# Holding the casts of early summed weights and of the second down group behind bank reads, and giving the down projection two more raw tiles

## The chip, the cores and the metric

The kernel runs on one core of a Trainium2 chip. The metric is the device time of one execution in microseconds, as the median of several runs. One execution was also recorded by the hardware profiler; the views of the profile quoted below come from that one.

## The reference

A two-layer encoder trunk: 1024 tokens of width 1024. Each layer mixes tokens (windowed attention in layer 0, a neighbourhood attention on a grid in layer 1), attends to a fixed memory, and then runs a SwiGLU feed-forward block of width 2816. The change lies in the feed-forward block:

```python
def rmsnorm(x, g):
    x32 = x.astype(jnp.float32)
    y = x32 * lax.rsqrt(jnp.mean(x32 * x32, axis=-1, keepdims=True) + EPS)
    return (y * g.astype(jnp.float32)).astype(x.dtype)
...
    for i in range(DEPTH):
        ...
        x = x + jnp.concatenate([y_tok, y_mem], axis=-1) @ w_out[i]
        h = rmsnorm(x, norm_ffn[i])
        gu = h @ w_gate_up[i]
        x = x + (jax.nn.silu(gu[..., :D_FF]) * gu[..., D_FF:]) @ w_down[i]
    return rmsnorm(x, norm_final)
```

## The kernel before

Activations are kept transposed: 8 tiles of 128 features, each in two token halves of 512 (`HS`). Every operand of a product is split into a high part, rounded by a cast on ACT (`hi`, L107), and the rest, by a subtraction on DVE (`lo`, L110); one product of two such operands is three matmuls (high x high, high x low, low x high).

The feed-forward products use a scheme of seven block products for a two by two block matrix product (products n = 0 to 6). Some of them read plain blocks, others sums and differences of blocks. For the gate and up projection the blocks of the weights are the left sides, those of the normalized activations the right sides:

- `right_sides()` makes `B[3]`, `B[2]`, `B[5]`, `B[4]`, `B[6]` step by step on DVE: normalize (L1291), subtract (L1288), then split into tiles named hT (`t_op`) or hB (`h_op`), four pieces each. `B[0]` and `B[1]` exist earlier.
- `Pair(j)` is a unit of 128 hidden features, j = 0 to 21. `prepare(n)` makes the weight of products n and n + 1: for n = 2 and n = 4 GpSimd forms sums of raw blocks in the tile wS (L1065, L1058), the n = 4 sums in place of the n = 2 sums; then `hi` and `lo` split the result. wS has two buffers, split weights (tag whl, names wgu, later wd) three, raw weights (tag raw) five. `load_gu()`, called by `prepare`, starts the load of a later raw tile on the SP queue.
- `product(n)` issues 12 matmuls into a PSUM bank X or Y (L1101), and `read(n)` takes the bank out: copies on ACT (L1112, L1118, L1121, L1126) or additions on DVE (L1109).
- Product 6 of two neighbouring units from the third pair on is itself split again (`Fourth`, matmuls L1183, reads L1211).

`order` lists the products. The first four units (`first`) run products 0 and 1 first, then two by two 3, 2, 5, 4, 6, each for both units. `gate_up()` walks through it, and prepares `lead` = 4 steps ahead. The scheduler of the framework sets the order on each engine from the code and its own estimates, so an operation of `prepare` may be placed earlier than it is written. Each engine takes its instructions in that order and waits at the first one that isn't ready.

The down projection has the same seven products, in the order 0, 1, 3, 2, 4, 5, 6, over six groups of hidden units (five of two, one of one). `left_side(i, g)` loads, combines and splits the weights of one group (raw tiles named wd_raw, kept blocks wd_kept), two groups ahead; `right_side` does it for the activations (b_raw, hB). Products i = 3 and i = 4 (the fourth and fifth) load two raw blocks and add or subtract them on DVE (L1429, L1435). `read` adds the banks to the residual on DVE (L1496). The dictionary `ahead` starts the first groups while the gate and up products still run: `left_side(0, 1)` three steps before their end.

Of the kernel before, what the change touches and what calls it, by code (L numbers as in the profile page):

```python
# [17 lines left out]
P = 128  # L18
D = 1024
# [22 lines left out]
def trunk_kernel(ctx: ExitStack, tc: tile.TileContext, a: dict, out: bass.AP):  # L42
# [61 lines left out]
        return phase[0].tile([P, D], F32, tag="raw", name=name, bufs=phase[2])  # L104

    def hi(dst, src):
        nc.scalar.copy(dst, src)  # L107

    def lo(dst, src, h, eng=None):
        (eng or nc.vector).tensor_tensor(dst, src, h.bitcast(F32), op=ALU.subtract)  # L110

    def load_w(src, tag="whl", bufs=3, eng=None, name="w", pool=wp, parts=1, raw=None):
        if raw is None:
# [428 lines left out]
    for layer in range(2):  # L542
# [467 lines left out]
        with (  # L1010
# [32 lines left out]
            class Pair:  # L1043


                def __init__(self, j):
                    self.j = j
                    self.left, self.raw, self.seen = {}, {}, set()

                def prepare(self, n):  # L1050

                    n -= n % 2
                    if n in self.left:
                        return
                    g1, g2 = self.raw[0][:, :HS], self.raw[0][:, HS:]
                    if n > 0:
                        u1, u2 = self.raw[1][:, :HS], self.raw[1][:, HS:]
                    sub = lambda o, p_, q_: nc.gpsimd.tensor_tensor(o, p_, q_, op=ALU.subtract)  # L1058
                    s = self.raw[0]
                    if n == 2:  # L1060
                        self.s = fs.tile([P, D], F32, tag="S", name="wS", bufs=2)
                    if n in (2, 4):
                        s = self.s
                    if n == 2:
                        nc.gpsimd.tensor_tensor(s[:, HS:], u1, u2, op=ALU.add)  # L1065
                        sub(s[:, :HS], s[:, HS:], g1)
                    if n == 4:
                        sub(s[:, HS:], g1, u1)
                        sub(s[:, :HS], g2, s[:, :HS])
                    if n == 0 and self.j < first:  # L1070
                        w = fp.tile([P, 2, D], F32R, tag="t8", name="wgu8", bufs=6)
                    elif n == 2 and self.j >= first:
                        w = fp.tile([P, 2, D], F32R, tag="w8", name="wgu2", bufs=1)
                    else:
                        w = wp.tile([P, 2, D], F32R, tag="whl", name="wgu", bufs=3)
                    if n == 6:
                        hi(w[:, 0, :HS], u2)
                        lo(w[:, 1, :HS], u2, w[:, 0, :HS])
                    else:
                        hi(w[:, 0], s)  # L1080
                        lo(w[:, 1], s, w[:, 0])
                    self.left[n], self.left[n + 1] = w[:, :, :HS], w[:, :, HS:]
                    if n == 4:
                        self.left[4], self.left[5] = self.left[5], self.left[4]
                    if n > 3 or (n == 0 and 2 <= self.j < first):
                        load_gu()
# [19 lines left out]
                def read(self, n):  # L1106
                    self.seen.add(n)
                    X, Y = self.X, getattr(self, "Y", None)
                    add = lambda o, p_, q_, op=ALU.add: nc.vector.tensor_tensor(o, p_, q_, op=op)  # L1109
                    if n == 0:  # L1110
                        self.g1 = temp("g1")
                        nc.scalar.copy(self.g1, X)  # L1112
                    elif n == 1:
                        add(self.g1, Y, self.g1)
                        nc.scalar.activation(self.g1, self.g1, AF.Silu)
                    elif n == 2:
                        self.g2 = temp("g2")
                        nc.scalar.copy(self.g2, X)  # L1118
                    elif n == 3:
                        self.c2 = temp("c2")  # L1120
                        nc.scalar.copy(self.c2, Y)  # L1121
                        if 4 in self.seen:
                            add(self.c2, self.c2, self.c1)
                    elif n == 4:
                        self.c1 = temp("c1")
                        nc.scalar.copy(self.c1, X)  # L1126
                        if 3 in self.seen:
                            add(self.c2, self.c2, self.c1)
                        if 5 in self.seen:
                            add(self.c2, self.c2, self.g2, ALU.mult)  # L1130
                    elif n == 5:
                        add(self.g2, Y, self.g2)
                        nc.scalar.activation(self.g2, self.g2, AF.Silu)
                        if 4 in self.seen:
                            add(self.c2, self.c2, self.g2, ALU.mult)
                    else:
                        add(self.c1, self.c1, X, ALU.subtract)
                        add(self.c1, self.c1, self.g1, ALU.mult)
# [3 lines left out]
            class Fourth:  # L1142
# [65 lines left out]
                def read(self, n):  # L1208
                    (a, b), X, Y = self.units, self.X, self.Y
                    low, high = slice(0, h2), slice(h2, HS)  # L1210
                    sub = lambda c, ps, op=ALU.subtract: nc.vector.tensor_tensor(c, c, ps, op=op)  # L1211
                    if n == "A":
                        sub(a.c1[:, low], X[:, low])
                        sub(a.c1[:, low], Y[:, low])
                    elif n == "B":
                        sub(a.c1[:, high], X[:, low])
                        sub(b.c1[:, high], Y[:, high])
                    else:
                        sub(
                            b.c1.rearrange("p (n c) -> p n c", n=2),  # L1220
                            X[:, low].unsqueeze(1).to_broadcast([P, 2, h2]),
                        )
                        sub(b.c1[:, low], X[:, high], ALU.add)
                        sub(b.c1, b.g1, ALU.mult)
                        sub(a.c1[:, high], Y[:, high])
                        sub(a.c1, a.g1, ALU.mult)
# [141 lines left out]
            def gate_up():  # L1368
                load_gu()
                for i, (u, n) in enumerate(order):  # L1370
                    if i + lead < len(order):
                        v, n_ = order[i + lead]
                        v.prepare(n_)
                    u.product(n)
                    u.read(n)
                    if i == 1:
                        norms[1].sums()
                    if i > 1:
                        run_some(rest, 2 if i == 2 or i >= 2 * first else 1)
                    if i >= 7 * first - 1:  # L1380
                        run_some(more, 1)
                    if n == "C":
                        hand_over(u.units[0].j // 2, *u.units)
                    elif n == 6 and u.j % 2:
                        hand_over(u.j // 2, us[u.j - 1], u)
                    yield i - len(order)
# [16 lines left out]
                    kept[g] = fp.tile([P, 2, 2, HS], F32, tag="t8", name="wd_kept", bufs=6)[:, :n]  # L1403
                    rows(kept[g][:, :, 0], g, 0, slice(0, HS))

            def left_side(i, g):

                p, n = groups[g]
                first_cols, second_cols = slice(0, HS), slice(HS, D)

                def raw():
                    return raw_tile("wd_raw").rearrange("p (n c) -> p n c", c=HS)[:, :n]

                if i == 0:
                    keep_rows(g)
# [7 lines left out]
                    nc.vector.tensor_tensor(a, b, a, op=ALU.subtract)  # L1423
                    src = a
                elif i == 3:
                    r, o = raw(), raw()
                    rows(r, g, 0, second_cols)
                    rows(o, g, 1, second_cols)
                    nc.vector.tensor_tensor(b, r, o, op=ALU.add)  # L1429
                    src = b  # L1430
                elif i == 4:
                    src, o = raw(), raw()
                    rows(src, g, 0, first_cols)
                    rows(o, g, 0, second_cols)
                    nc.vector.tensor_tensor(src, src, o, op=ALU.subtract)  # L1435
                elif i == 5:
                    src = raw()
                    rows(src, g, 1, first_cols)
                    nc.vector.tensor_tensor(src, src, a, op=ALU.subtract)
                else:  # L1440
                    src = raw()
                    rows(src, g, 1, second_cols)
                w = wp.tile([P, 2, D], F32R, tag="whl", name="wd", bufs=3)
                hi(two(w[:, 0], n), src)
                lo(two(w[:, 1], n), src, two(w[:, 0], n))
                for q in range(n):
                    left[i, p + q] = w[:, :, q * HS : (q + 1) * HS]

# [145 lines left out]
            }  # L1594
            for to_go in gate_up():
                for what, g in ahead.get(to_go, ()):
                    what(g) if what is keep_rows else what(0, g)
            norms = [Norm(row=None if is_a else next(factor_rows)), Norm()]
            ends = {c: Norm(HS // 2, 7) for c in quarter}
            dorder = [(i, g) for i in (0, 1, 3, 2, 4, 5, 6) for g in range(len(groups))]  # L1600
# [136 lines left out]
```

## Time and profile before

| | us |
|---|---|
| median of 3 runs | 2117.06 |
| lowest and highest | 2116.92, 2117.7 |
| the profiled execution | 2115.94 |
| its span, first to last instruction | 2114.2 |
| PE busy in the span | 2092.7 |
| DVE / ACT / POOL busy | 1524.6 / 1077.9 / 583.6 |

PE is TensorE's matmuls and PEld its weight loads, which run beside them; DVE is VectorE, ACT ScalarE, POOL GpSimd, SP the engine whose queue starts most transfers. The granted clock of TensorE is 0.998 over the span. Busy time counts an instruction from its start to its end and leaves out branches, semaphores and the issuing of transfers. A row of the timeline reads: start, duration, engine, line, operation, output and inputs, shape, count; in brackets the idle time of the engine before it and what ended that. A row of the waits reads: who waited for whom, then the total, how often, and the longest. The gate and up products run from about 393 to 815 us in layer 0 and from about 1466 to 1888 in layer 1, the down projection after them to about 1002 and 2102.

### The profile page before, as it was taken

How to read it: one execution, taken by the hardware profiler on the slowest of the kernel's cores; microseconds unless marked ns; L12 is line 12 of the kernel's file. 1: busy time of each engine (PE TensorE's matmuls, PEld its weight loads, DVE VectorE, ACT ScalarE, POOL GpSimd, SP SyncE). 2: the span in 40 equal slices, each digit the busy share in tenths (PEclk: the TensorE clock that was granted, in tenths of full speed). 3: DMA queues.
4: the chain of work that ended last, by engine and by line, in shares of the span. 5: the costliest groups of instructions: out<-in, count | busy, mean ns of one | idle time of the engine just before them, and what ended most of it. 6: DMA issues, size and time to landing. Idle time of an engine off the chain costs nothing.

```text
span 2114.2 us, 29053 instructions
## 1 busy us (share of the span) xinstructions
PE 2092.7 (99%) x10318; PEld 1750.1 (83%) x10318; DVE 1524.6 (72%) x2474; ACT 1077.9 (51%) x2037; POOL 583.6 (28%) x615
## 2 busy tenths in 40 slices
PE   9999999999999999999999999999999999999998
PEld 8788888888888888888888888888888888888887
DVE  7687886987666667776766666677986666677675
ACT  6687775544434335344466666664543434344443
POOL 0344330334444430000233223203243444400001
PEclk9999999999999999999999999999999999999999
DMA  6421128332333227866232222275232333267662
GB/s 232 146 82 51 36 83 288 99 115 100 110 108 111 91 105 254 313 216 207 78 110 68 69 72 78 64 266 157 75 110 105 110 115 104 91 254 256 205 221 95
DMA packets 121778, 288.08 MB, mean 136 GB/s; under 512 B 12705, under 2 KB 21153, under 8 KB 121633
## 3 DMA queue, kind: packets, MB, share of 16 engines
q1 hardware_dynamic: 113744, 272.42, 38.4%
q10 hardware_dynamic: 7888, 13.79, 1.7%
q8 instruction: 82, 1.34, 0.3%
q14 instruction: 64, 0.52, 0.1%
HBM read 211.19 MB, written 68.95 MB: 133 GB/s over the span
## 4 chain that ended last, share of the span: by engine, by line
PE 80%; issue 12%; DVE 3%; ACT 2%; POOL 2%; DMA 1%; POOLq 0%; ACTq 0%; SPq 0%; DVEq 0%
PE X L1101 16%; PE Y L1101 16%; PE mm L141 15%; PE po L141 8%; PE X L1532 5%; PE Y L1532 4%; PE O L809 3%; PE S L746 3%; PE pT L789 3%; PE X L1183 2%; PE Y L1183 2%; PE mm L448 1%; ACT p L761 1%; POOL wS L1058 1%; POOL wf L110 1%
## 5 line engine op out<-in xcount | busy, mean ns | idle before, releaser
L1101 PE MATMUL Y<-hB,wgu 128*128 128x512 f32 x1056 | 255.5, 391 | 0.8 <-ACT c L1121 0.8
L1101 PE MATMUL X<-hB,wgu 128*128 128x512 f32 x1056 | 254.8, 391 | 0.0
L1532 PE MATMUL X<-hB,wd 128*128 128x512 f32 (+1 forms) x1092 | 243.2, 383 | 0.9 <-DVE x L1496 0.9
L110 DVE TENSOR_TENSOR wgu<-wS,wgu 128x1024 fp32r<-128x1024 f32 (+1 forms) x124 | 155.4, 1253 | 120.9 <-ACT wgu L107 120.7
L1532 PEld LDWEIGHTS X<-hB,wd 128*128 128x128 f32 x1092 | 200.2, 188 | 41.4 <-issue 1.7
L1101 PEld LDWEIGHTS Y<-hB,wgu 128*128 128x128 f32 x1056 | 196.8, 188 | 43.4 <-ACT c L1121 1.6
L1101 PEld LDWEIGHTS X<-hB,wgu 128*128 128x128 f32 x1056 | 196.0, 188 | 39.8
L774 POOL TENSOR_SCALAR p<-p,stat 128x384 f32<-128x384 f32 (+1 forms) x256 | 143.1, 579 | 308.7 <-DVE stat L771 213.4
L141 PE MATMUL mm<-hT,wqk 128*128 128x512 f32 x672 | 199.3, 405 | 0.0
L107 ACT CAST wgu<-wS 128x1024 fp32r<-128x1024 f32 (+1 forms) x124 | 114.3, 923 | 142.0 <-POOL wS L1058 124.6
L141 PE MATMUL po<-yT,wo 128*128 128x512 f32 x768 | 184.2, 393 | 0.0
L1532 PE MATMUL Y<-hB,wd 128*128 128x512 f32 x792 | 180.4, 389 | 0.0
L1532 PEld LDWEIGHTS Y<-hB,wd 128*128 128x128 f32 x792 | 148.6, 188 | 31.2 <-DVE x L1496 0.4
L244 POOL TENSOR_TENSOR nr<-nv,neg_half 128x4 f32<-128x4 f32 (+1 forms) x12 | 13.3, 1105 | 582.9 <-DVE nv L243 573.7
L141 PEld LDWEIGHTS po<-yT,wo 128*128 128x128 f32 x768 | 142.7, 188 | 28.8 <-DVE yT L110 0.2
L1101 PE MATMUL X<-hT,wgu 128*128 128x512 f32 x624 | 150.2, 391 | 0.0
L107 ACT CAST hB<-b_raw 128x512 fp32r<-128x512 f32 x154 | 89.4, 618 | 115.5 <-DMA b_raw<-b_d 100.3
L1058 POOL TENSOR_TENSOR wS<-wgu_raw 128x512 f32<-128x512 f32 x44 | 61.2, 1391 | 292.1 <-DVE wgu L110 292.1
L1101 PEld LDWEIGHTS X<-hT,wgu 128*128 128x128 f32 x624 | 116.8, 188 | 26.3
L761 ACT ACTIVATE p<-p,stat 128x256 f32<-128x256 f32 (+1 forms) x192 | 112.4, 587 | 48.1 <-DVE stat L757 46.0
L110 DVE TENSOR_TENSOR pl<-pT,ph 128x384 fp32r<-128x384 f32 (+1 forms) x256 | 119.0, 493 | 19.1 <-ACT ph L107 15.9
L110 DVE TENSOR_TENSOR hB<-b_raw,hB 128x512 fp32r<-128x512 f32 x154 | 99.9, 687 | 42.2 <-ACT hB L107 42.1
(201 smaller groups left out, 4248.1 us busy)
## 6 DMA issues: line engine op xcount, KB each, us to landing
wgu_raw<-in_w_gu SPq DMA_DIRECT2D x92, 512.0 KB, 3.7
wd_raw<-in_w_dn SPq DMA_DIRECT2D x70, 512.0 KB, 4.4
b_raw<-b_d SPq DMA_DIRECT2D x70, 512.0 KB, 5.4
b_d<-c SPq DMA_DIRECT2D x88, 256.0 KB, 2.1
b_d<-t SPq DMA_DIRECT2D x66, 256.0 KB, 2.2
wo_raw<-in_w_out SPq DMA_DIRECT2D x32, 512.0 KB, 3.5
xr_d<-x ACTq DMA_DIRECT2D x32, 256.0 KB, 2.5
xr<-xr_d SPq DMA_DIRECT2D x16, 512.0 KB, 6.1
```

Source lines behind the costliest of these rows:

```text
L107: nc.scalar.copy(dst, src)
L110: (eng or nc.vector).tensor_tensor(dst, src, h.bitcast(F32), op=ALU.subtract)
L141: nc.tensor.matmul(ps[:, :n], l, r, start=start and i == 0 and j == 0, stop=stop and i == len(order) - 1 and j == 2,)
L746: nc.tensor.matmul(s_[:, :n], Q[self.h][:, qb * P : (qb + 1) * P], k, start=j == 0, stop=j == 1)
L761: nc.scalar.activation(p[:, :n], p[:, :n], AF.Exp, bias=m1, scale=-1.0, accum_out=s1)
L774: nc.gpsimd.tensor_scalar(p[:, :n], p[:, :n], ri[:, i : i + 1], 1.0, op0=ALU.mult, op1=ALU.mult)
L789: nc.tensor.transpose(tr[:, j * P : (j + 1) * P], p[:, j * P : (j + 1) * P], ident)
L809: nc.tensor.matmul(o[:, c0 : c0 + w * P], self.value(j), t[:, s0 : s0 + w].rearrange("p j q -> p (j q)"), start=j == js[0] and t is self.p ...
L1058: sub = lambda o, p_, q_: nc.gpsimd.tensor_tensor(o, p_, q_, op=ALU.subtract)
L1101: nc.tensor.matmul(ps, l, r, start=n in (0, 1, 3, 6) and k == 0 and i == 0, stop=k == 3 and i == 2, skip_group_check=True,)
L1183: nc.tensor.matmul(bank[:, at : at + h2], l, r, start=start and k == 0 and i == 0, stop=stop and k == 1 and i == 2, skip_group_check=True,)
L1532: nc.tensor.matmul(bank[:, c], l, r, start=i in (0, 1, 3, 6) and p == 0 and n == 0, stop=p == HF - 1 and n == 2, skip_group_check=True,)
```

## The change

1. `prepare` is cut in two. GpSimd's sums stay where they were; the split moves into a new function `split(n)`. For the first four units and n = 2 or 4 it is called one step after the sums, and its cast is pinned to its place in the program (`tc.keep_in_program_order`), so that the scheduler doesn't place it earlier. `load_gu()` moves with it.
2. `left_side(0, 1)`, the second group of the down projection, gets a list `behind`: its cast and its subtraction are issued after the last unit's copy of product 4 (`copied`) and after the read of step "B" (`summed`).
3. Products i = 3 and i = 4 of the down projection load their second block into one of two halves of a new tile wd_other (tag w8, the buffer that held the n = 2 weights of the later units) instead of a raw tile. (The product numbers of the short description count from one.)

```diff
     def hi(dst, src):
-        nc.scalar.copy(dst, src)
+        return nc.scalar.copy(dst, src)
...
                     if n == 4:
                         sub(s[:, HS:], g1, u1)
                         sub(s[:, :HS], g2, s[:, :HS])
+                    self.cast[n] = s
+                    if self.j >= first or n not in (2, 4):
+                        self.split(n)
+
+                def split(self, n, pin=False):
+
+                    n -= n % 2
+                    if n not in self.cast:
+                        return
+                    s, u2 = self.cast.pop(n), self.raw.get(1)
...
-                        hi(w[:, 0], s)
+                        ins = hi(w[:, 0], s)
+                        if pin:
+                            tc.keep_in_program_order(ins)
                         lo(w[:, 1], s, w[:, 0])
...
-                        nc.scalar.copy(self.c1, X)
+                        self.copied = nc.scalar.copy(self.c1, X)
...
-                        sub(b.c1[:, high], Y[:, high])
+                        b.summed = sub(b.c1[:, high], Y[:, high])
...
                         v.prepare(n_)
+                        if i >= 2 * first - lead:
+                            v, n_ = order[i + lead - 1]
+                            if v in us[:first]:
+                                v.split(n_, True)
...
+                def other():
+                    t = spare[g % 2].bitcast(F32)
+                    return t.rearrange("p (n c) -> p n c", c=HS)[:, :n]
...
                 elif i == 3:
-                    r, o = raw(), raw()
+                    r, o = raw(), other()
...
                 elif i == 4:
-                    src, o = raw(), raw()
+                    src, o = raw(), other()
...
-                hi(two(w[:, 0], n), src)
-                lo(two(w[:, 1], n), src, two(w[:, 0], n))
+                with ExitStack() as queued:
+                    for ins in behind:
+                        queued.enter_context(tc.issue_after(ins.ins))
+                    hi(two(w[:, 0], n), src)
+                    lo(two(w[:, 1], n), src, two(w[:, 0], n))
...
+                        left_side(0, g, (us[-1].copied, us[-1].summed) if g == 1 else ())
...
+            spare = fp.tile([P, 2, D], F32R, tag="w8", name="wd_other", bufs=1)
+            spare = spare[:, 0], spare[:, 1]
```

The order of PE's matmuls is the same in both kernels. On the other engines it differs at these places.

DVE, at the start of the gate and up products of layer 0 (layer 1 is alike). sq are squares for the norm, st and nv its means, g the gate's output, wgu a split weight, hT a piece of `B[3]` or `B[2]`. Before, ahead of the norm:

```order
L1264 TENSOR_TENSOR x<-po,x 128x512
L110 TENSOR_TENSOR wgu<-wS,wgu 128x1024
L230 TENSOR_TENSOR sq<-sq 128x512 x2
L1109 TENSOR_TENSOR g_4508<-Y,g_4508 128x512
L243 TENSOR_SCALAR nv<-st 128x4
```

and before, while `B[3]` and `B[2]` are made:

```order
L1109 TENSOR_TENSOR g_4602<-Y,g_4602 128x512
L1288 TENSOR_TENSOR x<-x 128x512
L110 TENSOR_TENSOR hT_4580<-x,hT_4580 128x512
L1288 TENSOR_TENSOR x<-x 128x512
L110 TENSOR_TENSOR hT_4631<-x,hT_4631 128x512
L1291 SCALAR_TENSOR_TENSOR x<-x,gains,bc 128x512 x2
```

After, at that second place:

```order
L1121 TENSOR_TENSOR g_4599<-Y,g_4599 128x512
L1300 TENSOR_TENSOR x<-x 128x512
L110 TENSOR_TENSOR hT_4580<-x,hT_4580 128x512
L110 TENSOR_TENSOR wgu<-wS,wgu 128x1024
L110 TENSOR_TENSOR hT_4628<-x,hT_4628 128x512
L1300 TENSOR_TENSOR x<-x 128x512
L110 TENSOR_TENSOR wgu<-wS,wgu 128x1024
L1303 SCALAR_TENSOR_TENSOR x<-x,gains,bc 128x512
```

Three subtractions of summed weights leave the end of the output projection; two of them now stand between the last piece of `B[3]` and the second piece of `B[2]`, the third behind the last piece of `B[2]`.

POOL at the same place. nr belongs to the norm of the second token half. Before:

```order
L1065 TENSOR_TENSOR wS<-wgu_raw 128x512
L1058 TENSOR_TENSOR wS<-wS,wgu_raw 128x512
L1058 TENSOR_TENSOR wS<-wgu_raw 128x512
L1058 TENSOR_TENSOR wS<-wgu_raw,wS 128x512
L1058 TENSOR_TENSOR wS<-wgu_raw 128x512
L1058 TENSOR_TENSOR wS<-wgu_raw,wS 128x512
L1065 TENSOR_TENSOR wS<-wgu_raw 128x512
L1058 TENSOR_TENSOR wS<-wS,wgu_raw 128x512
L244 TENSOR_TENSOR nr<-nv,neg_half 128x4
```

After:

```order
L1065 TENSOR_TENSOR wS<-wgu_raw 128x512
L1058 TENSOR_TENSOR wS<-wS,wgu_raw 128x512
L244 TENSOR_TENSOR nr<-nv,neg_half 128x4
L1058 TENSOR_TENSOR wS<-wgu_raw 128x512
L1058 TENSOR_TENSOR wS<-wgu_raw,wS 128x512
L1058 TENSOR_TENSOR wS<-wgu_raw 128x512
L1058 TENSOR_TENSOR wS<-wgu_raw,wS 128x512
L1065 TENSOR_TENSOR wS<-wgu_raw 128x512
L1058 TENSOR_TENSOR wS<-wS,wgu_raw 128x512
```

The n = 4 sums of the first two units and the n = 2 sum of the third unit, six operations, stand behind the norm instead of ahead of it.

DVE at the end of the gate and up products of layer 1, where the banks X and Y of the last split product 6 are read (c) and the second down group is split (the second wd row). Before:

```order
L110 TENSOR_TENSOR wd<-wd_kept,wd 128x1024
L1211 TENSOR_TENSOR c_17100<-c_17100,X_17220 128x256
L110 TENSOR_TENSOR wd<-wd_kept,wd 128x1024
L1211 TENSOR_TENSOR c_17100<-c_17100,Y_17221 128x256
L1109 TENSOR_TENSOR c_17216<-c_17216,c_17251 128x512
```

After:

```order
L110 TENSOR_TENSOR wd<-wd_kept,wd 128x1024
L1223 TENSOR_TENSOR c_17089<-c_17089,X_17209 128x256
L1223 TENSOR_TENSOR c_17089<-c_17089,Y_17210 128x256
L1121 TENSOR_TENSOR c_17205<-c_17205,c_17240 128x512
L1223 TENSOR_TENSOR c_17089<-c_17089,X_17209 128x256
L1223 TENSOR_TENSOR c_17240<-c_17240,Y_17210 128x256
L110 TENSOR_TENSOR wd<-wd_kept,wd 128x1024
```

The split of the second group has moved behind the four bank reads.

DVE in the down projection of layer 0, where product 2 ends and its banks are read (x). Before:

```order
L1435 TENSOR_TENSOR wd_raw<-wd_raw 128x1024
L110 TENSOR_TENSOR wd<-wd_raw,wd 128x1024
L1496 TENSOR_TENSOR x_00_8736<-X,xr 128x512
L1496 TENSOR_TENSOR x_10_8741<-X,xr 128x512
L1496 TENSOR_TENSOR x_20_8746<-X,xr 128x512
```

After:

```order
L110 TENSOR_TENSOR hB<-b_raw,hB 128x512 x2
L1519 TENSOR_TENSOR x_00_8729<-X,xr 128x512
L110 TENSOR_TENSOR wd<-wd_raw,wd 128x1024
L1519 TENSOR_TENSOR x_10_8734<-X,xr 128x512
L1519 TENSOR_TENSOR x_20_8739<-X,xr 128x512
L1519 TENSOR_TENSOR x_30_8744<-X,xr 128x512
```

The subtraction L1435 (L1455 after) no longer stands ahead of the reads, and the first read precedes the next split.

More of the change, by code (lines that the diff above doesn't have):

```diff
@@ L106, in hi @@
     def hi(dst, src):
-        nc.scalar.copy(dst, src)
+        return nc.scalar.copy(dst, src)
     def lo(dst, src, h, eng=None):
-        (eng or nc.vector).tensor_tensor(dst, src, h.bitcast(F32), op=ALU.subtract)
+        return (eng or nc.vector).tensor_tensor(dst, src, h.bitcast(F32), op=ALU.subtract)
     def load_w(src, tag="whl", bufs=3, eng=None, name="w", pool=wp, parts=1, raw=None):
@@ L1047, in __init__ @@
                     self.j = j
-                    self.left, self.raw, self.seen = {}, {}, set()
+                    self.left, self.raw, self.seen, self.cast = {}, {}, set(), {}
                 def prepare(self, n):
                     n -= n % 2
-                    if n in self.left:
+                    if n in self.left or n in self.cast:
                         return
@@ L1076, in prepare @@
                     if n == 6:
-                        hi(w[:, 0, :HS], u2)
-                        lo(w[:, 1, :HS], u2, w[:, 0, :HS])
-                    else:
-                        hi(w[:, 0], s)
+                        hi(w[:, 0, :HS], u2[:, HS:])
+                        lo(w[:, 1, :HS], u2[:, HS:], w[:, 0, :HS])
+                    else:
+                        ins = hi(w[:, 0], s)
+                        if pin:
+                            tc.keep_in_program_order(ins)
                         lo(w[:, 1], s, w[:, 0])
@@ L1404, in keep_rows, with left_side @@
                     rows(kept[g][:, :, 0], g, 0, slice(0, HS))
-            def left_side(i, g):
+            def left_side(i, g, behind=()):
                 p, n = groups[g]
@@ L1596, in trunk_kernel @@
                 for what, g in ahead.get(to_go, ()):
-                    what(g) if what is keep_rows else what(0, g)
+                    if what is keep_rows:
+                        keep_rows(g)
+                    elif what is left_side:
+                        left_side(0, g, (us[-1].copied, us[-1].summed) if g == 1 else ())
+                    else:
+                        what(0, g)
+            spare = fp.tile([P, 2, D], F32R, tag="w8", name="wd_other", bufs=1)
+            spare = spare[:, 0], spare[:, 1]
             norms = [Norm(row=None if is_a else next(factor_rows)), Norm()]
```

## Prediction

> **What bounds the kernel now.** I read the page first, then the waits of PE and of its weight loads, then windows of the one stretch that the change fills up, then the timeline row by row in it. From the page:
>
> ```profile
> span 2114.2 us, 29053 instructions
> PE 2092.7 (99%) x10318; PEld 1750.1 (83%) x10318; DVE 1524.6 (72%) x2474; ACT 1077.9 (51%) x2037; POOL 583.6 (28%) x615
> ```
>
> PE is busy for 2092.7 of 2114.2 us, so all idle time together is 21.5 us. A change that leaves the matmuls alone can win only the part of it that its own waits hold. The waits of PE that belong to the touched code (total, times, longest), and below them those of the weight loads in front of the same matmuls:
>
> ```profile
> PE Y L1183 <- DVE c L1211: 1.5, 1, 1.5
> PE X L1532 <- DVE x L1496: 0.9, 1, 0.9
> PE Y L1101 <- ACT c L1121: 0.8, 2, 0.4
> ...
> PEld Y L1183 <- DVE c L1211: 1.7, 1, 1.7
> PEld X L1532 <- issue: 1.7, 3, 1.3
> PEld Y L1101 <- ACT c L1121: 1.6, 2, 0.8
> ```
>
> That is 3.2 us by the matmuls, 4.6 us by the weight loads if one takes the longest for X. The share of DVE over the span (72%) hides where it is full. Two windows, one per layer, from the first right side of the second token half to the weight of product 5 of the second unit pair (columns: length, then busy time and instructions of PE, PEld, DVE, ACT, POOL):
>
> ```profile
> 404.35:460.68 56.33, 55.95 (x242) 44.97 (x240) 53.75 (x70) 28.68 (x46) 15.28 (x10) 1.00 0.22 71
> 1476.69:1533.00 56.31, 55.93 (x242) 45.05 (x240) 53.93 (x70) 28.67 (x46) 15.36 (x10) 1.00 0.22 70
> ```
>
> DVE has 56.33 - 53.75 = 2.6 us free in layer 0 and 2.4 in layer 1. The rows at both ends show that PE follows it there:
>
> ```profile
> 423.73 5.76 PE L1101 MATMUL X<-hT,wgu 128*128 128x512 f32 x24
> 425.07 0.69 DVE L110 TENSOR_TENSOR hT<-x,hT 128x512 fp32r<-128x512 f32 x1 [0.64 <-ACT hT L107]
> ...
> 458.98 1.77 DVE L110 TENSOR_TENSOR wgu<-wS,wgu 128x1024 fp32r<-128x1024 f32 x1 [0.69 <-ACT wgu L107]
> 460.81 2.15 PEld L1101 LDWEIGHTS Y<-hB,wgu 128*128 128x128 f32 x10 [0.20 <-DVE wgu L110]
> ```
>
> The first pair: the last piece of right side B[2] is ready at 425.76, and its product, begun at 423.73, needs it with its 11th matmul (10 x 0.24 us later, about 426.1): 0.3 us to spare. The second pair: the weight of that product 5 is ready at 460.75 and the load waits for it. What DVE gets to do on top in this window, beyond its free time, moves PE.
>
> **The early summed weights: DVE work moved into the full window.** Before, three summed weights (twice n = 2, once n = 4) are split while the output projection still runs:
>
> ```profile
> 387.88 1.22 DVE L110 TENSOR_TENSOR wgu<-wS,wgu 128x1024 fp32r<-128x1024 f32 x1
> 394.99 2.15 DVE L110 TENSOR_TENSOR wgu<-wS,wgu 128x1024 fp32r<-128x1024 f32 x1 [0.47 <-ACT wgu L107]
> ...
> 428.08 1.22 DVE L110 TENSOR_TENSOR wgu<-wS,wgu 128x1024 fp32r<-128x1024 f32 x1
> 429.22 1.29 DVE L110 TENSOR_TENSOR hB<-x,hB 128x512 fp32r<-128x512 f32 x2
> ```
>
> After, all three subtractions stand inside the window, two of them ahead of the last piece of B[2]. Each takes 429.22 - 428.08 = 1.14 us of the queue: 3.4 us a layer. The three casts that go with them cost ACT 3 us of a queue that is half idle in the window (28.68 of 56.33): nothing by itself. What leaves the old place is worth little: the subtraction at 394.99 held the last sums of squares, for which the means' weight load waited 0.5 us in layer 0, of which I count 0.3 as an earlier start of the window; layer 1 has no such wait.
>
> ```profile
> PEld st L223 <- DVE sq L230: 0.5, 1, 0.5
> ```
>
> With the casts, GpSimd's sums move. The n = 4 sums overwrite the tile that the n = 2 split reads, so they cannot begin before it is done. Before, six GpSimd operations (both n = 4 sums and the n = 2 sum of the third unit, first and last quoted) ran ahead of the window:
>
> ```profile
> 389.18 1.68 POOL L1058 TENSOR_TENSOR wS<-wgu_raw 128x512 f32<-128x512 f32 x1 [11.81 <-DVE wgu L110]
> 398.97 1.60 POOL L1058 TENSOR_TENSOR wS<-wS,wgu_raw 128x512 f32<-128x512 f32 x1
> ```
>
> After, they stand behind the subtractions, all six in the window. What that costs a full DVE is read from two places where it happens already:
>
> ```profile
> 417.06 1.89 DVE L1288 TENSOR_TENSOR x<-x 128x512 f32<-128x512 f32 x3
> ...
> 435.31 1.29 POOL L1065 TENSOR_TENSOR wS<-wgu_raw 128x512 f32<-128x512 f32 x1 [33.47 <-DMA wgu_raw<-in_w_gu]
> 435.59 3.87 DVE L110 TENSOR_TENSOR hT<-x,hT 128x512 fp32r<-128x512 f32 x3
> 436.69 1.63 POOL L1058 TENSOR_TENSOR wS<-wS,wgu_raw 128x512 f32<-128x512 f32 x1
> 442.89 1.68 POOL L1058 TENSOR_TENSOR wS<-wgu_raw 128x512 f32<-128x512 f32 x1 [4.58 <-DVE wgu L110]
> 443.93 1.20 DVE L1109 TENSOR_TENSOR c<-c,g 128x512 f32<-128x512 f32 x1
> 444.54 1.73 POOL L1058 TENSOR_TENSOR wS<-wgu_raw,wS 128x512 f32<-128x512 f32 x1
> 445.04 2.31 DVE L110 TENSOR_TENSOR wgu<-wS,wgu 128x1024 fp32r<-128x1024 f32 x1
> ```
>
> Three DVE operations of that size take 1.89 us alone and 3.87 beside two of GpSimd: 2.0 us lost. At 443 it is (1.20 - 0.69) + (2.31 - 1.22) = 1.6. I take 1.8 for each pair, three pairs: 5.4 us a layer. The bounds are nothing (if the sums fall beside operations that are not held) and the six operations' whole length, about 10 us (six of 1.3 to 1.75).
>
> The sum for one layer, at the weight of product 5: layer 0 gives 3.4 + 5.4 - 2.6 free, less 0.3 for an earlier start, so +5.9; layer 1 3.4 + 5.4 - 2.4 = +6.4. This uses up all free time and adds none, so by these prices it is a floor. New waits could add something: the third cast stands ahead of right-side casts on ACT and waits for GpSimd's n = 4 sum, two operations of some 1.7 us after the first subtraction. ACT's other rows cover part of those 3.4 us, so I allow 0 to 2 us a layer, an estimate, and take 0. On the SP queue the loads of two later raw tiles wait for those sums too; their first reader, the third unit's n = 2 sum, stands behind the third subtraction anyway.
>
> **Bank reads ahead of casts.** The Y wait of 0.4 us a layer comes from this row, whose cast waits for GpSimd while the copy behind it would free the bank:
>
> ```profile
> 455.98 1.05 ACT L107 CAST wgu<-wS 128x1024 fp32r<-128x1024 f32 x1 [8.63 <-POOL wS L1058]
> 457.56 5.81 PE L1101 MATMUL Y<-hB,wgu 128*128 128x512 f32 x24 [0.38 <-ACT c L1121]
> ```
>
> The first copy now stands ahead of two of those casts, so the wait goes. It lies before the weight wait at 460.81, and my sum is taken there, so it is no further gain.
>
> **The second down group.** In layer 1:
>
> ```profile
> 1879.98 1.05 ACT L107 CAST wd<-wd_kept 128x1024 fp32r<-128x1024 f32 x1 [1.37 <-DMA wd_kept<-in_w_dn]
> 1881.06 1.23 DVE L110 TENSOR_TENSOR wd<-wd_kept,wd 128x1024 fp32r<-128x1024 f32 x1 [1.35 <-ACT wd L107]
> 1882.67 0.97 PE L1183 MATMUL Y<-hT,wgu 128*128 128x256 f32 x6 [1.53 <-DVE c L1211]
> ```
>
> DVE waits for a cast that waits for a DMA, and the bank read is queued behind it. After, all four bank reads stand ahead: -1.5 (0 to -1.7). The split comes a few us later, which is covered: the down projection starts with the first group,
>
> ```profile
> 1888.38 3.81 PE L1532 MATMUL X<-hB,wd 128*128 128x512 f32 x16
> ```
>
> and works on it for 24 matmuls (24 x 0.23 = 5.5 us) before it wants the second.
>
> **Two raw tiles more.** In layer 0 a subtraction waits for a raw tile and holds the read of bank 0:
>
> ```profile
> 932.08 1.22 DVE L1435 TENSOR_TENSOR wd_raw<-wd_raw 128x1024 f32<-128x1024 f32 x1 [2.38 <-DMA wd_raw<-in_w_dn]
> 935.18 15.02 PE L1532 MATMUL X<-hB,wd 128*128 128x512 f32 x65 [0.87 <-DVE x L1496]
> ```
>
> With operands loaded into a tile of their own the subtractions run earlier and the first bank read precedes the next split: -0.9 (0 to -1.3). The new loads stand early on SP, ahead of five right-side loads; their tile was last read by the gate products, so they need not wait. SP's transfers are no fewer and no more.
>
> **Sum.** 5.9 + 6.4 - 1.5 - 0.9 = +9.9 us against the profiled execution's 2115.94, that is 2125.8. That execution lies 1.1 below the median of 2117.06, so I forecast 2117.06 + 9.9 = 2127.
>
> [...]
>
> **Rivals.** (1) The stretch is not paid: the sums fall beside DVE rows that are not held, or DVE's free time takes them. Then 3.4 - 2.6 - 0.3 and 3.4 - 2.4 give +1.5, less 2.4: 2116, no change. For it: a DVE read of PSUM inside a GpSimd operation runs at its usual 0.69,
>
> ```profile
> 393.05 1.75 POOL L1058 TENSOR_TENSOR wS<-wgu_raw 128x512 f32<-128x512 f32 x1
> 393.83 0.69 DVE L1264 TENSOR_TENSOR x<-po,x 128x512 f32<-128x512 f32 x1 [0.19 <-PE po L141]
> ```
>
> and the window has such rows. Against: most of its rows are sums and subtractions within SBUF, like those at 435. (2) Faster: the extra DVE work finds cover wholly, since right sides may be ready earlier than used. Then only waits go: at the weight loads' prices 1.7 + 1.3 + 1.6 + 0.5 = 5.1, 2112. It decides if B[2] has 5 us to spare; the rows at 423.73 and 425.07 say 0.3. (3) Each GpSimd operation holds DVE for its whole length: 10 us instead of 5.4, 2117.06 + 9.9 + 2 x 4.6 = 2136. Against: the 2.0 beside 2.9.
>
> **Chances.** Forecast 0.70 (2121 to 2133: half the 5.4 us in both layers, 2127 - 5.4, up to 6 us for three pairs and 2 us of new waits, 2127 + 1.2 + 4), rival 1 0.17, rival 2 0.06, rival 3 0.07. 0.2% is 4.2 us, about what a measurement of this kernel can tell from no change. Faster by more: rival 2, 0.06. Within: rival 1 and the low edge of the forecast, 0.21. Slower: 0.73. The range 2115 to 2133 leaves out rivals 2 and 3 and little of the rest; the forecast's own range is 2121 to 2133.
>
> **What would show it.** In the profile after: PE or its loads waiting at the X products about 424 us and again up to 466 us, for DVE hT, hB or wgu; DVE without idle time from 404 to 466; six GpSimd sums more in that window; the same in layer 1; the waits on L1211 and L1496 gone. If PE waits nowhere between 420 and 470, the step on DVE is wrong; if it waits for ACT casts instead, the new waits were the larger part.

## The result and the profile after

| | before | after |
|---|---|---|
| median of 6 runs each, us | 2117.09 | 2125.46 |
| lowest to highest | 2115.7 to 2117.7 | 2125.4 to 2127.17 |
| profiled execution's span | 2114.2 | 2123.3 |

The ratio is 1.004, with a 95% interval of 1.003 to 1.0051: the kernel is slower by 8.4 us (6 to 11). The forecast was 2127.0 in a range of 2115 to 2133, with a chance of 0.73 for slower.

The page of the changed kernel, first its span and busy times:

```profile
span 2123.3 us, 29027 instructions
PE 2098.0 (99%) x10318; PEld 1751.5 (82%) x10318; DVE 1520.8 (72%) x2474; ACT 1078.7 (51%) x2037; POOL 595.5 (28%) x615
```

PE has the same 10318 matmuls and is busy 5.3 us longer than before (2092.7); its idle time is 25.3 us against 21.5. So less than half of the loss of 9.1 us in the span shows as waiting. The rest is in busy rows, among them matmuls that run slower, to which I come below. The waits of PE in the touched code (total, times, longest), all of them, and two of those of its weight loads, the largest and the one for the weight of product 5:

```profile
PE X L1113 <- DVE hB L110: 3.5, 2, 1.8
...
PE X L1113 <- DVE hT L110: 1.4, 2, 0.7
PE X L1113 <- ACT c L1138: 1.1, 2, 0.6
...
PE X L1113 <- ACT hT L107: 1.0, 2, 0.5
...
PE X L1195 <- DVE c L1223: 0.2, 1, 0.2
...
PEld X L1113 <- DVE hB L110: 4.3, 2, 2.2
...
PEld Y L1113 <- DVE wgu L110: 0.9, 2, 0.6
```

The three waits of before that belonged to this code (Y for the read L1211, X for the read L1496, Y for the copy L1121) are gone. In their place PE waits once per layer for pieces of the right sides: hT is `B[2]`, hB is `B[4]`. These are the X products that the prediction named. In layer 0, in the timeline (start, duration, idle time before it and what ended that):

```profile
424.96 0.49 PE L1113 MATMUL X<-hT,wgu 128*128 128x512 f32 x1 [0.52 <-ACT hT L107]
426.17 4.43 PE L1113 MATMUL X<-hT,wgu 128*128 128x512 f32 x17 [0.72 <-DVE hT L110]
...
442.45 1.43 PE L1113 MATMUL X<-hB,wgu 128*128 128x512 f32 x5 [1.78 <-DVE hB L110]
444.42 7.18 PE L1113 MATMUL X<-hT,wgu 128*128 128x512 f32 x24 [0.54 <-ACT c L1138]
```

The last row is new: 24 matmuls take 7.18 us where before the same product took 5.75, without a pause ahead of it:

```profile
440.22 5.75 PE L1101 MATMUL X<-hT,wgu 128*128 128x512 f32 x24
```

Windows of that stretch and of the product behind it, and of the same product in layer 1 (the third column from the end is the granted clock), show that it came with a lower clock:

```profile
435.90:444.40 8.50, 6.20 (x25) 4.16 (x23) 8.50 (x9) 3.02 (x6) 6.58 (x4) 0.97 0.19 63
444.40:451.40 7.00, 6.98 (x24) 5.66 (x25) 7.00 (x9) 2.45 (x3) 3.38 (x2) 0.79 0.35 115
1522.30:1529.60 7.30, 7.22 (x24) 5.75 (x25) 7.30 (x10) 2.50 (x4) 3.38 (x2) 0.77 0.29 108
```

After the two pauses of 1.78 and 0.54 us the granted clock is 0.79 over one product, in layer 1, after 1.67 and 0.56 us, 0.77: 1.4 and 1.65 us that no wait lists.

The prediction summed up one window per layer: from the first right side of the second token half on DVE to the end of the subtraction that makes the weight of product 5 of the second unit pair. For after (columns: length, then busy time and instructions of PE, PEld, DVE, ACT, POOL, and the granted clock, DMA share and GB/s):

```profile
403.45:466.07 62.62, 58.97 (x242) 45.66 (x240) 58.53 (x72) 31.14 (x49) 29.49 (x15) 0.97 0.26 80
1481.53:1544.03 62.50, 59.05 (x242) 45.72 (x240) 58.41 (x72) 31.13 (x49) 29.48 (x15) 0.97 0.24 80
```

The window is 62.62 and 62.50 us long; before, taken in the same way (404.35 to 460.75 and 1476.69 to 1532.99), 56.40 and 56.30. That is +6.2 in both layers, and the prediction's terms for it, without the earlier start, add up to +6.2 and +6.4 (3.4 + 5.4 - 2.6 and - 2.4). But the inside of the window is not as predicted. DVE's busy time grew by 4.5 to 4.7 us, not by 8.8, and 4.1 us of the window are idle on DVE, not none. Nearly all of the idle time is one piece:

```profile
458.64 1.22 DVE L110 TENSOR_TENSOR wgu<-wS,wgu 128x1024 fp32r<-128x1024 f32 x1
459.94 1.29 POOL L1065 TENSOR_TENSOR wS<-wgu_raw 128x512 f32<-128x512 f32 x1 [3.69 <-DVE wgu L110]
462.63 2.00 ACT L107 CAST wgu<-wS 128x1024 fp32r<-128x1024 f32 x2 [4.82 <-POOL wS L1058]
463.71 2.36 DVE L110 TENSOR_TENSOR wgu<-wS,wgu 128x1024 fp32r<-128x1024 f32 x2 [3.85 <-ACT wgu L107]
```

A subtraction frees a buffer of wS, GpSimd forms the fifth unit's n = 2 sum in it, a cast of that sum stands on ACT ahead of the cast that product 5 needs, and only then does DVE go on. So the sum came out, and two of its terms did not. The experiments had to find out which.

### The profile page after: what moved, and what is told of

It reads as the page before. It is cut to its first block, busy times and chain, and to the rows that moved or that the text cites. A ratio compares the mean times of both kernels' runs of the same rounds, so it can differ in the third digit from the quotient of the medians.

```text
span 2123.3 us, 29027 instructions
## 1 busy us (share of the span) xinstructions
PE 2098.0 (99%) x10318; PEld 1751.5 (82%) x10318; DVE 1520.8 (72%) x2474; ACT 1078.7 (51%) x2037; POOL 595.5 (28%) x615
## 4 chain that ended last, share of the span: by engine, by line
PE 78%; issue 12%; DVE 5%; ACT 2%; POOL 1%; DMA 0%; POOLq 0%; ACTq 0%; DVEq 0%
PE X L1113 16%; PE Y L1113 15%; PE mm L141 14%; PE po L141 8%; PE X L1555 5%; PE Y L1555 4%; PE O L809 3%; PE S L746 3%; PE pT L789 3%; PE X L1195 2%; PE Y L1195 2%; DVE x L1300 1%; DVE wgu L110 1%; ACT p L761 1%; PE mm L448 1%
## 5 line engine op out<-in xcount | busy, mean ns | idle before, releaser
L1113 PE MATMUL X<-hT,wgu 128*128 128x512 f32 x624 | 154.8, 398 | 3.6 <-DVE hT L110 1.4
```

Of the source, the lines that this page charges most:

```text
L1113: nc.tensor.matmul(ps, l, r, start=n in (0, 1, 3, 6) and k == 0 and i == 0, stop=k == 3 and i == 2, skip_group_check=True,)
```

## The experiments

Each kernel was timed in five rounds beside the kernel before. The chips differed (before had medians of 2118.1, 2117.85 and 2119.11 there), so times are compared as ratios to before, whose intervals are about plus or minus 0.1%, or 2 us. The window length in the trace, from one recorded execution of each kernel, repeats better: it agrees to 0.2 us between the layers except in `e9` and `e11`. So it decides; "theory 1" is the prediction's ledger. The expectations for `e1`, `e2`, `e3` and `e6` give times on the scale of 2117.1. The later ones start from the medians of `e1` (2114.0) and `e4` (2115.1) as they were timed, 0.9 and 0.8 us above their ratios on that scale, so there the difference from `e1` or `e4` is what counts.

| kernel | ratio to before, interval | window, layers 0 and 1 | DVE busy in it |
|---|---|---|---|
| before | 1 | 56.40, 56.30 | 53.82, 53.92 |
| after | 1.0040 (1.0030 to 1.0051) | 62.62, 62.50 | 58.53, 58.41 |
| `e1` parts 2 and 3 alone | 0.9981 (0.9972 to 0.9990) | 56.36, 56.41 | 53.80, 54.01 |
| `e2` part 1 alone | 1.0055 (1.0042 to 1.0068) | 62.73, 62.58 | 58.64, 58.51 |
| `e3` after, sums in place | 1.0040 (1.0027 to 1.0052) | 61.19, 61.23 | 56.72, 56.74 |
| `e6` the same and a tile more | 1.0035 (1.0022 to 1.0049) | 60.59, 60.60 | 58.79, 58.80 |
| `e7` e1 + three subtractions | 1.0016 (1.0007 to 1.0025) | 58.97, 59.03 | 57.20, 57.15 |
| `e8` e1 + six sums | 1.0018 (1.0009 to 1.0027) | 59.46, 59.49 | 57.99, 58.00 |
| `e9` e1 + both | 1.0051 (1.0039 to 1.0064) | 62.91, 63.77 | 61.53, 61.30 |
| `e4` e1, second pair's casts held | 0.9987 (0.9979 to 0.9996) | 56.20, 56.31 | 51.07, 51.27 |
| `e10` e4 + three subtractions | 1.0012 (1.0003 to 1.0021) | 58.96, 58.97 | 54.47, 54.45 |
| `e11` e4 + six sums | 1.0008 (0.9999 to 1.0017) | 59.39, 60.43 | 55.27, 55.35 |
| `e12` e4 + both | 1.0049 (1.0037 to 1.0062) | 62.84, 62.89 | 58.85, 58.88 |

**The parts one by one.** `e1` splits every summed weight at once, as before, and keeps parts 2 and 3:

```diff
-                    if self.j >= first or n not in (2, 4):
+                    if True:
                         self.split(n)
```

> The second down group and the raw tiles alone; the early summed weights are split where the kernel before splits them. The prediction prices these two parts at -1.5 and -0.9: 2117.1 - 2.4 = 2114.7. The profile of the changed kernel shows -1.7 (end of the gate products of layer 1) and -1.2 (down projection of layer 0), which gives 2114.2. Rival: these waits only vanish because PE comes later in the changed kernel; then 2116.5 to 2117.5, and waits on the bank reads are back.

It is the fastest kernel of the study: 0.9981, 4 us below before by the ratio (2 to 6). By the traces the stage from the first gate product of layer 1 to the first down product is 420.77 us instead of 422.02, and in layer 0 the time from the first down product to the next norm is 190.44 instead of 191.59: -1.25 and -1.15. Of the waits in the touched code one is left in the list:

```profile
PE Y L1113 <- ACT c L1133: 0.8, 2, 0.4
```

So both waits together were worth what they showed (2.4 us), without part 1 too; the rival falls. `e2` is the other half, with `left_side(0, g)` and two raw tiles for i = 3 and 4 as before:

> The early summed weights alone. By the prediction 2117.1 + 5.9 + 6.4 = 2129.4; by the shifts in the profile of the changed kernel (about +5.9 and +6.2 before the other parts) 2128.5 to 2129.2. Rival: the parts hide each other, so that the loss alone is below 8 us: under 2125.

1.0055, or +11.6 us (9 to 14), and windows of 62.7 and 62.6 us. The whole loss is part 1; the parts do not hide each other.

**Taking the sums out of the window.** `e3` writes the n = 4 sums of the first two units in place, so that they need not wait for the n = 2 split; `e6` also gives the third unit's n = 2 sum a free tile (the last piece of the diff, in `e6` alone):

```diff
-                    if n == 4:
+                    if n == 4 and self.j < 2:
+                        s = self.raw[0]
+                        sub(g1, g1, u1)
+                        sub(g2, g2, self.s[:, :HS])
+                    elif n == 4:
                         sub(s[:, HS:], g1, u1)
...
-                    if n == 4:
+                    if n == 4 and self.j > 1:
                         self.left[4], self.left[5] = self.left[5], self.left[4]
...
-                        self.s = fs.tile([P, D], F32, tag="S", name="wS", bufs=2)
+                        if self.j == 2:
+                            self.s = fp.tile([P, 2, D], F32R, tag="w8", name="wS8", bufs=1)[:, 0].bitcast(F32)
+                        else:
+                            self.s = fs.tile([P, D], F32, tag="S", name="wS", bufs=2)
```

> As the changed kernel, but the n = 4 sums of the first two units are written in place over their raw blocks instead of over the n = 2 sums, so they no longer wait for the n = 2 split and run ahead of the full window. DVE, ACT and SP keep their order. Four of six moved GpSimd operations leave the window; two (the n = 2 sum of the third unit) stay. Theory 1 (the prediction's prices, 1.8 us of DVE for a pair of sums): 2 x 1.8 less per layer, 2125.5 - 7.2 = 2118.3. Theory 2 (the sums cost DVE only some 1.4 us a layer; the place of the three subtractions ahead of the right sides and the waits behind it cost the rest): at most 1.4 a layer, 2122.5 to 2125.

> As the kernel before it in this list, and the n = 2 sum of the third unit goes into a tile of its own: all six moved GpSimd operations run ahead of the window, while the three subtractions stay inside it. Theory 1: 3.4 - 2.6 - 0.3 = +0.5 in layer 0 and 3.4 - 2.4 = +1.0 in layer 1, less 2.4 to 2.9 for the other parts: 2115.7 to 2116.2. Theory 2: the free time lies behind the pieces that PE waits for, so the subtractions cost nearly their whole 3.4 us, less some 0.9 of an earlier start, with or without sums: +2.5 to +4 a layer, 2119 to 2122.

Theory 1 is missed in both: scaled to 2117.1 the ratios give 2125.6 and 2124.5, and of theory 2's ranges only the upper ends, 2125 and 2122, reach into the intervals (2122.8 to 2128.1 and 2121.8 to 2127.5). The windows became shorter, by 1.3 to 1.4 us in `e3` and 1.9 to 2.0 in `e6`, but the times hardly moved. In `e6`, layer 0, the timeline shows two reasons:

```profile
381.27 1.75 POOL L1058 TENSOR_TENSOR wgu_raw<-wgu_raw,wS 128x512 f32<-128x512 f32 x1
434.30 1.84 POOL L1068 TENSOR_TENSOR wS<-wgu_raw 128x512 f32<-128x512 f32 x1 [30.02 <-DMA wgu_raw<-in_w_gu]
...
385.37 5.73 PE L141 MATMUL po<-yT,wo 128*128 128x512 f32 x24 [1.12 <-DVE wo L110]
```

The n = 4 sums ran early (the second at 367.26, the last to 383.0 us), and beside them DVE's rows of the output projection grew (one of L273 at 367.77 us took 1.78 us, while two at 371.82 took 1.40), for which PE waited: 2.7 us there in both layers together, 1.7 in `e3`, none in after. And the third unit's sum did not leave the window at all, because its raw tile came in only when the raw block used in place was free. So four of six sums moved, not six, and most of what they gave back (3.9 us of window in `e6`, 2.7 in `e3`) was paid in the stage before. As a test of the price the pair is inconclusive; it shows that these sums were not free in the place tried ahead of the window.

**Adding the suspected costs, one at a time.** `e7`, `e8` and `e9` go the other way. They start from `e1`, where nothing has moved, and add operations that write a tile which nothing reads. The diff is that of `e9`; `e7` has the calls of `difference` alone, `e8` those of `sums`:

```diff
+                more = fp.tile([P, 2, D], F32R, tag="w8", name="more", bufs=1)
+
+                def difference():
+                    src = made[0].bitcast(F32)
+                    o = nc.vector.tensor_tensor(more[:, 0], src[:, 0], src[:, 1], op=ALU.subtract)
+                    tc.keep_in_program_order(o)
+
+                def sums(src, n):
+                    t = more[:, 1].bitcast(F32)
+                    src = src.bitcast(F32)
+                    for i in range(n):
+                        nc.gpsimd.tensor_tensor(t[:, i % 2 * HS :][:, :HS], src[:, 0], src[:, 1], op=ALU.add)
...
                     B[3][k] = pair(t, t_op(k))
+                    if k > 1:
+                        difference()
+                    if k == 3:
+                        sums(B[3][3], 4)
                     yield
...
                     sub(b21, t, b21)
+                    if k == 3:
+                        difference()
+                    if k == 3:
+                        sums(B[2][3], 2)
                     yield
```

> The kernel of the second down group and the raw tiles alone (2114.0), with three subtractions of 128x1024 added on DVE in each layer, at the places where the changed kernel has the three moved ones; they write a tile that nothing reads. No cast, sum or load moves. Theory 1 (free time of DVE takes what it can): 3.4 - 2.6 and 3.4 - 2.4, 2115.8. Theory 2 (the free time lies behind the pieces of B[2] and B[4] that PE waits for): two of them, 2.3 us, stand ahead of B[2] with some 0.9 us to spare, all three, 3.4 us, ahead of B[4]: +2 to +3.4 a layer, 2118 to 2121.

> The same kernel (2114.0) with six sums of 128x512 added on GpSimd in each layer, four behind the last piece of B[3] and two behind the last piece of B[2], where the changed kernel has its moved sums; they write a tile that nothing reads. DVE, ACT and SP keep their order. Theory 1 (1.8 us of DVE for a pair): 5.4 - 2.6 and 5.4 - 2.4, 2119.8. Theory 2 (the sums are cheap: 1.4 us a layer or less, within the free time): 2114 to 2115.

> Both additions at once. Theory 1: 8.8 - 2.6 and 8.8 - 2.4, 2126.6, or 12.6 above the kernel without additions. Theory 2: the sum of what the two do alone, or less, since a sum beside a delayed DVE finds other rows to stretch: 2118 to 2123. What is left to the changed kernel's own 11.4 us above 2114.0 belongs to the chain from GpSimd's sums over casts to the second pair's weights, which neither addition touches.

Three subtractions alone make the window 2.6 us longer, six sums 3.1, both 6.5 and 7.4. For the sums theory 1's number holds (+2.8 and +3.0 forecast), and theory 2 falls. For the subtractions it doesn't: +0.8 and +1.0 were forecast. DVE's busy time shows how: `e7` adds 3.4 and 3.1 us of it, but DVE's free time takes up only 0.8 in layer 0 (window less busy: 2.56 in `e1`, 1.77 in `e7`) and 0.5 in layer 1. Theory 2's range of times holds, though not its place. PE does not wait at `B[2]`, but mainly at a copy (2.31 us) that is queued behind a cast that waits for GpSimd, as at 455.98 in the prediction, and then loses 1.5 us at a lower clock: 7.34 us instead of the 5.83 of before, at a granted clock of 0.76 from 1538.5 to 1545.7 us:

```profile
1538.50 7.34 PE L1113 MATMUL Y<-hB,wgu 128*128 128x512 f32 x24 [2.31 <-ACT c L1133]
```

By the ratios the three kernels are 7.4, 7.8 and 14.8 us above `e1`, by the windows of both layers 5.2, 6.2 and 13.9. For both additions that lies nearer to theory 1's 12.6 than to theory 2's 4 to 9, though theory 1 was wrong on the subtractions. It is no less than the changed kernel's own 12.5 over `e1`, so nothing is left over for the chain that the expectation names.

How sums and DVE hinder each other, in `e8`, layer 1:

```profile
1492.43 4.03 DVE L1300 TENSOR_TENSOR x<-x 128x512 f32<-128x512 f32 x3
...
1488.97 6.34 POOL L1319 TENSOR_TENSOR more<-hT 128x512 f32<-128x512 f32 x4 [12.86 <-DVE hT L110]
1502.68 9.86 POOL L1319 TENSOR_TENSOR more<-hT 128x512 f32<-128x512 f32 x2 [7.37 <-DVE hT L110]
```

Beside the first four sums, 6.34 us for two pairs, three DVE rows take 4.03 us instead of the 1.89 of `e1`. The last two take long themselves: 9.86 us for a pair that takes 3.0 to 3.5 elsewhere in this trace, while DVE's rows keep their usual lengths for most of that time (0.69 us for one of 128x512 up to 1510.2, then 1.19 and 1.77).

**The changed kernel's own queue order.** In the changed kernel the second pair's casts stand behind the copies of Y. `e4` has only this: `split` is deferred and pinned for the third and fourth unit alone.

```diff
-                    if self.j >= first or n not in (2, 4):
+                    if self.j not in (2, 3) or n not in (2, 4):
...
-                            if v in us[:first]:
+                            if v in us[2:first]:
```

> The kernel of the second down group and the raw tiles alone (2114.0), and the early summed weights are held and pinned for the third and fourth unit only, where no sum and no subtraction moves into the full window: the copy of bank Y comes ahead of the cast. The prediction's step: no further gain, since the wait for the weight of product 5 stands behind it: 2113.5 to 2114.5. Rival: the wait on the copy, 0.4 us by the matmuls and 0.8 by the weight loads in each layer, comes off: 2112.4 to 2113.2. A third way: the subtraction of that weight, now behind three of DVE's rows, is later: 2114.5 to 2117.

The window is unchanged (56.20, 56.31) and so is the time within the intervals (0.9987 against 0.9981). The wait on the copy is gone, and one on the weight of product 5 has taken its place:

```profile
PE Y L1113 <- DVE wgu L110: 0.7, 2, 0.3
```

That is the prediction's step. But the inside changed: DVE is busy 51.3 us instead of 54.0, and idle for 5.0, mostly in one piece that is already that of the changed kernel:

```profile
1531.98 2.36 DVE L110 TENSOR_TENSOR wgu<-wS,wgu 128x1024 fp32r<-128x1024 f32 x2 [3.87 <-ACT wgu L107]
```

So this is the kernel with which the load in the changed kernel's window is to be compared. `e10`, `e11` and `e12` add the same operations to it.

> The kernel with the third and fourth unit's casts held (2115.1), with the three subtractions of the earlier run added on DVE in each layer. There they cost some 4.1 us a layer in the gate products: 0.7 at a copy of bank X, 1.9 at the copy of bank Y behind a cast that waits for GpSimd's sum, and 1.5 by a lower granted clock after that pause. Here that copy is ahead of the cast. Theory 1 (once nothing blocks, DVE's free time takes 2.4 to 2.6 of the 3.4): +0.8 to +1 a layer, 2116.7 to 2117.1. Theory 2 (the subtractions cost their place whatever stands on ACT): +3.4 a layer or more, 2121 to 2124.

> The same kernel (2115.1) with the six added sums on GpSimd in each layer. On the kernel without held casts they cost 3.1 us a layer in the gate products, against 2.8 and 3.0 by the prediction's price. If that price is one of DVE time, it is the same here: +3 a layer, 2121. If it came from the copy of bank Y (0.7 of the 3.1 showed there): +2.3 a layer, 2119.7.

> The same kernel (2115.1) with both additions: the same number of DVE and GpSimd operations in the full window as in the changed kernel, the same order of copies and casts of the second pair, but no cast or sum moved. If the load alone explains the loss: +5.8 to +6.4 a layer, as in the changed kernel (75.4 and 75.3 us from the first gate product to product 4 of the second unit pair's second unit, against 69.1 without), 2126.5 to 2128. If the moved chain from sums over casts to weights adds a part of its own: 2 to 3 us less, 2123 to 2125.

The windows of `e4` and `e10`, layer 1, of `e12`, both layers, and of `e11`, layer 0 (the third column from the end is the granted clock):

```profile
1478.03:1534.34 56.31, 56.02 (x242) 45.05 (x240) 51.27 (x69) 28.77 (x46) 13.33 (x9) 1.00 0.22 70
```

```profile
1480.73:1539.70 58.97, 56.83 (x242) 44.81 (x240) 54.45 (x72) 28.47 (x46) 14.27 (x9) 1.00 0.22 67
```

```profile
405.09:467.93 62.84, 58.04 (x242) 44.62 (x240) 58.85 (x72) 28.37 (x46) 31.17 (x15) 1.00 0.20 63
1482.66:1545.55 62.89, 59.30 (x242) 45.55 (x240) 58.88 (x72) 28.50 (x46) 31.75 (x15) 0.97 0.20 63
```

```profile
404.06:463.45 59.39, 56.81 (x242) 44.90 (x240) 55.27 (x69) 28.91 (x46) 29.95 (x15) 1.00 0.23 67
```

Three subtractions cost 2.7 us of window again, whatever stands on ACT, though no longer by the wait on the copy of Y; the time (+5.3 us over `e4` by the ratios) lies between the two theories. Six sums cost 3.2 in layer 0 and 4.1 in layer 1, which speaks for +3 a layer; but by the ratios `e11` is only 4.4 us above `e4`, which fits the lower forecast (+2.3 a layer). The two do not agree, and why stays open. Both cost 6.6 in each layer (13.1 us by the ratios), against 6.2 to 6.4 for the changed kernel over `e4`. And `e12` has the changed kernel's waits on DVE at the X products, with no cast or sum of the first pair moved:

```profile
PE X L1113 <- DVE hB L110: 3.5, 2, 1.8
PE X L1113 <- DVE hT L110: 1.4, 2, 0.7
```

Load on DVE in this window, three subtractions and six sums, is thus enough for the whole loss; a further cost by a chain of the moved sums and casts is not needed. The added sums read other tiles than the moved ones, so the runs do not show what each moved operation costs by itself.

## Why the prediction was right, and where it was not

- **Place and mechanism.** Right. PE's new waits lie at the X products of `B[2]` and `B[4]`, in both layers, and adding the same load to a kernel without the move (`e12`) brings the same waits for DVE there and the same window to 0.4 us.
- **The sum at the weight of product 5.** +5.9 and +6.4 were forecast. In layer 0 it is 466.07 - 460.75 = +5.3; in layer 1 the window is 6.2 longer. The start of layer 0's window is 0.9 earlier instead of 0.3.
- **Three subtractions, 3.4 us.** Right as work on DVE: 3.1 to 3.4 in `e7` and `e10`.
- **Six sums, 5.4 us.** Too much: this is one mis-sized term. From `e4` to after DVE's busy time grows by 58.41 - 51.27 = 7.1 us in layer 1 and by 7.5 in layer 0; less 3.4 for the subtractions that leaves 3.7 and 4.1. Added alone they cost 4.0 to 4.2 (`e8`, `e11`). That is 1.2 to 1.4 us a pair instead of 1.8. One of the moved sums, at 429.79 in after, takes 8.19 us itself, and the DVE rows beside it keep their lengths up to 437.34 (three in 1.88 us, three in 1.89); that this makes the pairs cheaper is an estimate.
- **DVE's free time, -2.6 and -2.4.** Too much: this is the other. From `e4` to after only about 1 us of it was used up (5.04 idle in layer 1, then 4.09). Most of the idle time is one wait in a chain from DVE over GpSimd and ACT back to DVE, 3.87 us in `e4` and 3.86 in after (layer 1), there 6.2 us later in the window: it moved with the work ahead of it and was no reserve. "DVE without idle time from 404 to 466" was wrong for that reason.
- **These two errors cancel.** 3.4 + 5.4 - 2.5 = 6.3 forecast; 3.4 + 3.7 - 1.0 = 6.1 by the runs in layer 1, for 62.50 - 56.31 = 6.2 measured (the 3.7 is what the subtractions leave of DVE's growth, so this only divides the measured sum). The total was better than its terms, and that was luck: with the subtractions alone the same ledger missed, in `e7` and `e10`, by 1.6 to 1.9 us of window a layer.
- **New waits, allowed for with 0 to 2 us and taken as 0.** PE does wait for ACT at these products, 2.1 us in all, but behind DVE: in layer 0 the cast of `B[2]` had itself waited 1.29 us for DVE, and the copy of X came after the pause for `B[4]`. The windows contain these waits.
- **The clock.** Not in the prediction. 1.4 and 1.65 us of what PE lost in after came as a lower granted clock after its pauses (0.79 and 0.77). It is no further term of the window above, and the window comes out as long without it: part 1 alone (`e2`) takes 62.73 us in layer 0, where the product of 24 behind the pauses took 5.85 us, and 62.58 in layer 1, where it took 6.86; `e12` takes 62.84 at a granted clock of 1.00 and 62.89 at 0.97. In `e12`, layer 0, PE waits 1.28 us for the weight of product 5 instead, which it does not in after. Only in `e9` and `e11`, where in layer 1 the product of `B[2]` was already slower (its last 17 matmuls in 5.77 us against 4.40 in layer 0 in `e9`, its last 14 in 5.07 against 3.52 in `e11`, there at a granted clock of 0.72), is that layer's window 0.9 and 1.0 us longer than layer 0's.
- **Bank reads ahead of casts, no gain.** Right (`e4`), and by the reason given: the weight of product 5 stands behind it.
- **Second down group, -1.5; raw tiles, -0.9.** Right: the traces of `e1` give -1.25 and -1.15, and in after these waits are gone.
- **Rival 3, each sum holding DVE for its whole length.** Fell with the price of 1.2 to 1.4 us for a pair that runs some 3 us; no run shows the 10 us. Its objection, 2.0 beside 2.9, is that of the rows at 435 us: DVE 3.87 instead of 1.89, beside GpSimd's 1.29 + 1.63. The sums are dearer than rival 1 had it (nothing): `e8`, `e11`. Rival 2 needed 5 us to spare at `B[2]`, and PE waited there.

The version to keep is `e1`: parts 2 and 3 without part 1.

## What to carry to other kernels

Idle time of a nearly full engine need not be a reserve: look at what ended each gap. Here it was a chain that begins with the engine's own work, and the gap moved along (3.87 us in `e4`, 3.86 in after) and saved only 1 us of 5. Before work is deferred into a later stretch, add the same number of operations there to the old kernel, writing to a tile that nothing reads: such kernels gave here the prices that the ledger had got right only in sum. And make the parts of a change one at a time: two of three were gains, and the third hid them.

## What the hardware showed that was not expected

Some pauses of PE cost more than their length. After 1.78 + 0.54 us of waiting (after, layer 0) one product of 24 matmuls ran at a granted clock of 0.79 (7.18 us instead of 5.75). After 2.31 us (`e7`, layer 1) one took 7.34 us at 0.76 instead of 5.83; in `e11`, layer 1, after only 1.18 + 0.66, the granted clock was 0.72 from the first pause to the end of that product and its last 14 matmuls took 5.07 us, while in `e8` they took 3.52 behind the same two pauses. And in `e12`, layer 0, the product of 24 took 5.84 us, at a granted clock of 1.00 over the window, behind 1.71 + 0.50 us. So pauses of about the same length were followed by a lower clock in one trace and not in another; what decides it is not shown here.

Where a GpSimd sum and DVE rows meet, it was not always DVE that took longer, as it was in the prediction's rows at 435 us (3.87 us instead of 1.89). In after, layer 0, it was GpSimd:

```profile
429.79 8.19 POOL L1065 TENSOR_TENSOR wS<-wgu_raw 128x512 f32<-128x512 f32 x1 [7.29 <-DVE wgu L110]
...
432.52 1.88 DVE L1300 TENSOR_TENSOR x<-x 128x512 f32<-128x512 f32 x3
434.33 1.89 DVE L110 TENSOR_TENSOR hB<-x,hB 128x512 fp32r<-128x512 f32 x3
```

One sum takes 8.19 us instead of 1.3 (1.27 at 440.58, in layer 1 8.18 at 1507.87), and the DVE rows shown beside it, three in 1.88 and three in 1.89 us, take what three take alone (1.89 in the prediction's row at 417.06).
